# Down groups of parts two and three: four weight pairs by seven products instead of three, and another order of the products

## The chip, the cores and the metric

The kernel runs on one core of a Trainium2 chip. The metric is device time in microseconds (us), the median of three runs. All arithmetic is in float32; a float32 factor is split into a high and a low part (type fp32r), and a product of two such factors takes three matmuls: high by high, low by high, high by low. The engines that matter here: TensorE (PE) does the matmuls, ScalarE (ACT) makes the high parts by a cast, VectorE (DVE) makes the low parts by a subtraction and adds tiles, SyncE (SP) and GpSimd (POOL) issue the loads. Each engine works through its own instructions in order and waits for semaphores of the others.

## The reference

One decoder block on 256 tokens of width 2048: a half-step feed-forward network (FFN), a mixer of two kinds of heads, a second half-step FFN, a gated embedding and a last norm. Only the FFNs are touched:

```python
def swiglu(x, w_gu, w_down):
    gate, up = jnp.split(x @ w_gu, 2, axis=-1)
    return (jax.nn.silu(gate) * up) @ w_down
h = h + 0.5 * swiglu(rms_norm(h, ffn1_norm[i]), ffn1_w_gu[i], ffn1_w_down[i])
```

The inner width is 5632, which is 11 blocks of 512 columns.

## The kernel before

**Groups.** An FFN is worked through in three parts of 3, 4 and 4 inner blocks (`PARTS`). A part has one gate/up group for each of its blocks, and then two down groups, with `nb` 0 and 2; each down group makes two of the four output blocks of 512 columns from the part's inner blocks. The rows of the down weights that belong to one part come in pairs of 2 x 128 rows: 6 pairs in part one, 8 in parts two and three. A group writes four PSUM banks: two blocks of columns by two halves of the tokens.

**Plain pairs and products.** A plain pair (lines 541 to 552) is one weight tile `raw` of 128 x 1024: loaded by SP (line 74), cast by ACT to `whi` (line 77), subtracted by DVE to `wlo` (line 78), and used by 12 matmuls of 512 columns. For two blocks of columns one pair index costs two plain pairs, 24 matmuls. The first `ns` pair indices of a group are done instead by Strassen's scheme: the 2 x 2 blocks (two halves of the tokens by two rows of a pair, and two rows by two blocks of columns) take seven products instead of eight, so 7 x 3 = 21 matmuls for each pair index. `ns` is 4 for gate/up groups (`NS`), and for down groups 2 in part one and 3 in parts two and three (`NS_DOWN`).

**What a product needs.** All `ns` pairs of one product go together: its weights are one tile `R` of 128 x (512 ns), a quarter of the weights, or a sum of quarters that DVE (line 307) or an adding DMA (line 314) has made in place; ACT casts it to `shi` (line 298) and DVE subtracts to `slo` (line 299). There are two buffers each for `shi` and `slo`, so the weights of a product can only be cast once the product two places ahead has done its last matmul. Products 0, 4 and 6 take the left side as it is (4 is A12, the first half of the tokens with the second rows of the pairs). Products 1, 2, 3 and 5 take sums of left sides, `Sh` and `Sl`, which `halves` makes from the hidden blocks `hTh`, `hTl`: for down groups of parts two and three one pair index at a time (line 539), an inner block giving two indices. Behind products 0 and 1 ACT copies the result to another bank (line 347), behind products 2 and 3 ACT copies it to `part` (line 350) and DVE subtracts that from another bank (line 352).

**What sets the order.** `plan` puts the products of a group between the plain pairs of the group before it: behind plain pairs 1 to 7 of the last gate/up group of parts two and three stand the seven products of that part's first down group, in the order `SEVEN` = 0, 1, 2, 4, 3, 5, 6. Generators in `Lanes` are advanced one step behind each plain pair; they make the sums for the left sides and bring each hidden block (`down_input`) through two DMAs into `hTh` and `hTl`. In the first down group the plain pairs that use the last hidden block stand last (line 265). What is written so is then put in order by a scheduler, engine by engine, except for instructions marked `keep_in_program_order`.

Of the kernel before, what the change touches and what calls it, by code (L numbers as in the profile page):

```python
# [26 lines left out]
PARTS = ((0, 3), (3, 7), (7, 11))  # L27


NS = 4  # L30
NS_DOWN = tuple(3 if i1 - i0 == 4 else 2 for i0, i1 in PARTS)


SEVEN = (0, 1, 2, 4, 3, 5, 6)


W_IN_ORDER = (2, 0, 4, 3, 1, 5, 8, 10, 12, 9, 11, 13, 6, 7)
# [9 lines left out]
def block_kernel(ctx, tc, a, out):  # L47
# [15 lines left out]
    lanes = Lanes(4)  # L63
# [184 lines left out]
    class Group:  # L248
# [8 lines left out]
        def __init__(self, kind, part, src, quarters, ns, bank, nb=0):  # L257
            self.kind, self.part, self.src, self.ns, self.nb, self.bank = kind, part, src, ns, nb, bank
            self.quarters, self.raw, self.first = quarters, {}, False
            self.last = part == len(PARTS) - 1  # L260
            self.banks = self.follower = None
            self.plain = [(b, g) for b in range(2) for g in range(ns, len(src[0]))]
            if kind == "dn" and nb == 0:

                self.plain.sort(key=lambda x: x[1] >= len(src[0]) - 2)
            elif kind == "behind":

                self.plain.sort(key=lambda x: x[1] // 2)
            self.sums = self.all_sums()
# [20 lines left out]
        def all_sums(self):  # L290

            fp = current[0]

            def halved(j, b):
                w = self.raw[j, b]
                hi = fp.tile([P, NS, NB], F32R, tag="shi", name="shi", bufs=2)[:, 0:self.ns]
                lo = fp.tile([P, NS, NB], F32R, tag="slo", name="slo", bufs=2)[:, 0:self.ns]
                keep(nc.scalar.copy(hi, w))  # L298
                nc.vector.tensor_tensor(out=lo, in0=w, in1=hi, op=ALU.subtract)  # L299
                return hi, lo  # L300

            def keep(ins):

                return tc.keep_in_program_order(ins) if self.first == "2" else ins

            def add(x, y):
                keep(nc.vector.tensor_tensor(out=self.raw[x], in0=self.raw[x], in1=self.raw[y], op=ALU.add))  # L307

            def add_loaded(x, y):


                if self.first:
                    return add(x, y)
                nc.gpsimd.dma_start(out=self.raw[x], in_=self.quarters[y[1]][y[0]], accum_op=ALU.add)

            for i in SEVEN:
                ws = halved(*((0, 0), (0, 0), (0, 0), (0, 1), (1, 0), (1, 1), (0, 0))[i])
                if i == 0:
                    add((0, 0), (0, 1))
                    add_loaded((0, 1), (1, 1))  # L320
                elif i == 1:
                    add((0, 0), (1, 1))
                elif i == 2:
                    add_loaded((0, 0), (1, 0))
                yield ws
# [28 lines left out]
    def plan(n):  # L354


        def sources(name, blk):

            q, pairs = a[name + "q"][blk], a[name][blk]
            return [q[:, :, g, :].rearrange("j p n -> p j n") for g in range(q.shape[2])] + \  # L360
                [pairs[g] for g in range(pairs.shape[0])], q

        groups = []
        for p, (i0, i1) in enumerate(PARTS):
            for i in range(i0, i1):
                plain = PLAIN[n]
                if i < plain:
                    src = [([a[f"w_gu{n}0"][2 * i + b][g] for g in range(KD // 2)], None) for b in range(2)]
                else:
                    src = [sources("w_gu" + n, 2 * (i - plain) + b) for b in range(2)]  # L370
                groups.append(Group("gu", p, [x[0] for x in src], [x[1] for x in src], NS if i >= plain else 0,
                                    len(groups) % 2))
            for nb in (0, 2):
                src = [sources(f"w_down{n}{p}", nb + b) for b in range(2)]
                groups.append(Group("dn", p, [x[0] for x in src], [x[1] for x in src], NS_DOWN[p], len(groups) % 2, nb))
        if n == "2":
            src = [sources("w_behind", b) for b in range(2)]
            groups.append(Group("behind", len(PARTS), [x[0] for x in src], [x[1] for x in src], NS_BEHIND,
                                len(groups) % 2))
        if n == "1":  # L380

            groups[0].plain.sort(key=lambda x: x[1])
        made, carried = [], []
        for i, group in enumerate(groups):
            group.follower = follower = groups[i + 1] if i + 1 < len(groups) else None
            after = groups[i + 2] if i + 2 < len(groups) else None
            n_plain = len(group.plain)
            at, loads, carried = [], {0: carried}, []
            if follower is not None and follower.ns:
                first = 8 if not group.ns else 4 if follower.kind == "behind" else \  # L390
                    1 if group.kind == follower.kind or group.part and follower.kind == "dn" else 2
                at = [min(first + j, n_plain - 1) for j in range(7)]
                if not group.ns:
                    follower.first = n

                    loads.setdefault(max(at[0] - 5, 0), []).extend(follower.loads())
                if after is not None and after.ns:
                    *three, last = after.loads(follower)
                    for x, one in zip((4, 5, 6), three):
                        loads.setdefault(at[x], []).append(one)  # L400
                    carried = [last]
            todo = []
            for j, (b, g) in enumerate(group.plain):
                todo.append(("plain", (b, g)))
                order.append(("pair", group.src[b][g]))
                if group.kind == "behind" and g == KD // 2 - 1:
                    order.append(("pair", a["w_pp"][b]))
                for x in range(7):
                    if at and at[x] == j:
                        todo.append(("seventh", x))  # L410
                        order.append(("sum", follower))
                order.extend(loads.get(j, []))
            made.append((group, todo))
        return made
# [8 lines left out]
    def halves(kind, his, los, ns, wait=0, at_once=2):  # L423
# [19 lines left out]
        for g0 in range(0, ns, at_once):  # L443
            n = min(at_once, ns - g0)
            k0 = 2 * (g0 % 2)
            hi, lo = (x[g0 // 2][:, k0:k0 + 2 * n] for x in (his, los))
            keep = lambda ins: ins
            if g0 == 2 and n == 1:

                keep = tc.keep_in_program_order  # L450
                yield
            if n == 2:
                x = fp.tile([P, 2 * NB], F32, tag="sil", name="S")
            else:
# [14 lines left out]
    def ffn(n, nT, r, scale, next_norm, stat):  # L469
        xs = picker(*nT)  # L470
        late = callable(r)
        with tc.tile_pool(name="ffn", bufs=1) as fp:
            hTh, hTl = [], []
# [42 lines left out]
            for group, todo in ffn_plan[n]:  # L516
# [5 lines left out]
                if dn and group.nb and not group.last:  # L522
                    lanes.add(1, halves("gu", *nT, NS))
                elif dn and group.nb and group.follower:
                    lanes.add(1, halves("behind", *nxt, NS_BEHIND, 4))
                elif not dn and group.follower.kind == "dn" and not group.part:
                    lanes.add(1, halves("dn", hTh[i0:], hTl[i0:], NS_DOWN[group.part]))
                if dn and group.last and nxt is None:
                    nxt = new_nT()
                if group.banks is None:  # L530
# [1 line left out]
                for kind, one in todo:  # L532
                    if kind == "seventh":
                        follower = group.follower
                        follower.product(SEVEN[one])
                        if group.part and not dn and one == 5 and follower.kind == "gu" and \
                                follower.follower.kind == "dn":
                            p = PARTS[group.part][0]
                            lanes.add(1, halves("dn", Later(hTh, p), Later(hTl, p), NS_DOWN[group.part], 0, 1))
                        continue  # L540
                    b, g = one
                    whi, wlo = next_weights()
# [29 lines left out]
                    else:  # L572
# [7 lines left out]
                        hTl.append(tl)  # L580
                        i0, i1 = PARTS[group.part]

                        last = (3 if i1 - i0 == 4 else 2) if len(hTh) == i1 else 0
                        gen = down_input(outs, sil, th, tl, last)
                        next(gen)

# [762 lines left out]
def _layout(i):  # L1349
    f = {k: np.asarray(v) for k, v in i.items()}  # L1350
    m = {}
# [5 lines left out]
    for n in "12":  # L1357
        b = _blocks(f[f"ffn{n}_w_gu"][0])
        nb = DFF // NB
        b = np.stack([b[:nb], b[nb:]], axis=1).reshape(b.shape)  # L1360
        m[f"w_gu{n}0"] = np.ascontiguousarray(b[:2 * PLAIN[n]])
        _parted(m, f"w_gu{n}", b[2 * PLAIN[n]:], NS)
        b = _blocks(f[f"ffn{n}_w_down"][0])
        for p, (i0, i1) in enumerate(PARTS):
            _parted(m, f"w_down{n}{p}", b[:, 2 * i0:2 * i1], NS_DOWN[p])
    _parted(m, "w_behind", _blocks(f["ple_w_gate"][0])[0:2], NS_BEHIND)
    w = f["w_in"][0]
    m["w_in"] = _blocks(np.concatenate([w[:, :4096], w[:, 4112:]], axis=1))
# [29 lines left out]
```

## Time and profile before

| | us |
|---|---|
| median of 3 runs (1944.40 to 1944.83) | 1944.74 |
| the profiled execution's own time | 1945.28 |
| its span, first to last instruction | 1943.6 |
| PE busy, 8884 matmuls | 1928.1 |
| DVE busy | 1570.4 |
| ACT busy | 1164.1 |
| POOL busy | 148.4 |

A matmul of 512 columns is listed with about 0.39 us, but the next one starts 0.227 us behind it, since they overlap. The places of this text in the profiled span, for the first FFN: part two has its last gate/up group from 339.2 to 375.3 us, its first down group to 416.8 and its second to 463.0; in part three the last gate/up group runs from 586 to 622 and the first down group to 663.5. The second FFN has the same stages at 1482 to 1606 and from 1729 on. In the rows below a number in brackets at the end is the idle time of the engine just before, and the instruction that ended it.

### The profile page before, as it was taken

The page shows a single profiled execution, that of the slowest core. Times are in us where ns is not written, and L with a number is a line of the kernel's source. Part 1 is how long each engine was busy: PE and PEld are TensorE (multiplying, and loading weights), DVE is VectorE, ACT ScalarE, POOL GpSimd, SP SyncE. Part 2 cuts the span into 40 slices and gives each one's busy share as a digit, 9 for nine tenths or more (in the row PEclk, how much of TensorE's full clock was granted, in tenths as well). Part 3 has the DMA queues.
Part 4 walks back from the last instruction along what each step waited for, and adds up shares of the span by engine and source line. Part 5 has one row for each costly group of instructions (what it writes and reads, how often), then busy time and mean ns, then how long its engine had stood idle before and what let it go on. Part 6 is the DMA issues. An engine that isn't in the chain of part 4 may idle for free.

```text
span 1943.6 us, 24163 instructions
## 1 busy us (share of the span) xinstructions
PE 1928.1 (99%) x8884; PEld 1594.0 (82%) x8884; DVE 1570.4 (81%) x1703; ACT 1164.1 (60%) x1362; POOL 148.4 (8%) x226
## 2 busy tenths in 40 slices
PE   9999999999999999999999999999999999999998
PEld 7888888888888888878788888888888888888886
DVE  7879878997789766797856579899888987888865
ACT  6656666666666557664555456566556755657654
POOL 0010110000010000010100000010000100001000
PEclk9999999999999999999999999999999999999999
DMA  8778898888888765556565776788888987989764
GB/s 307 269 236 282 252 293 285 237 288 249 280 285 242 228 218 171 176 169 211 161 213 159 244 283 231 226 281 289 248 275 241 327 264 244 271 237 314 234 214 143
DMA packets 144182, 475.05 MB, mean 244 GB/s; under 512 B 19648, under 2 KB 47296, under 8 KB 129856
## 3 DMA queue, kind: packets, MB, share of 16 engines
q1 hardware_dynamic: 107200, 302.16, 44.4%
q0 software_dynamic: 25920, 160.44, 30.2%
q10 hardware_dynamic: 10944, 10.91, 1.8%
q8 instruction: 69, 1.13, 0.2%
q14 instruction: 49, 0.40, 0.1%
HBM read 451.44 MB, written 22.02 MB: 244 GB/s over the span
## 4 chain that ended last, share of the span: by engine, by line
PE 92%; DVE 5%; DMA 2%; issue 1%; ACT 0%; POOL 0%; SPq 0%; POOLq 0%; DVEq 0%; ACTq 0%
PE d L550 5%; PE d L552 5%; PE d L551 5%; PE u L551 5%; PE u L552 5%; PE u L550 5%; PE g L343 5%; PE g L342 5%; PE g L344 5%; PE g L551 4%; PE g L552 4%; PE pj L112 4%; PE pj L113 4%; PE pj L114 4%; PE g L550 4%; PE d L344 3%
## 5 line engine op out<-in xcount | busy, mean ns | idle before, releaser
L77 ACT CAST whi<-raw 128x1024 fp32r<-128x1024 f32 (+1 forms) x489 | 511.3, 1049 | 401.1 <-PE pj L114 106.6
L78 DVE TENSOR_TENSOR wlo<-raw,whi 128x1024 fp32r<-128x1024 f32 (+1 forms) x489 | 592.0, 1218 | 162.9 <-ACT whi L77 161.8
L299 DVE TENSOR_TENSOR slo<-R,shi 128x2048 fp32r<-128x2048 f32 (+2 forms) x224 | 444.9, 1989 | 132.1 <-ACT shi L298 130.1
L298 ACT CAST shi<-R 128x2048 fp32r<-128x2048 f32 (+2 forms) x224 | 373.9, 1671 | 141.5 <-DVE R L307 62.7
L112 PE MATMUL pj<-whi,nTh 128*128 128x512 f32 x448 | 179.4, 401 | 0.0
L113 PE MATMUL pj<-wlo,nTh 128*128 128x512 f32 x448 | 175.2, 391 | 1.1 <-DVE wlo L78 1.1
L114 PE MATMUL pj<-whi,nTl 128*128 128x512 f32 x448 | 174.9, 390 | 0.0
L550 PE MATMUL d<-whi,hTh 128*128 128x512 f32 x448 | 174.5, 390 | 0.0
L551 PE MATMUL d<-wlo,hTh 128*128 128x512 f32 x448 | 174.4, 389 | 0.0
L552 PE MATMUL d<-whi,hTl 128*128 128x512 f32 x448 | 173.4, 389 | 0.0
L551 PE MATMUL g<-wlo,nTh 128*128 128x512 f32 x400 | 156.6, 391 | 0.6 <-DVE wlo L78 0.6
L552 PE MATMUL g<-whi,nTl 128*128 128x512 f32 x400 | 156.0, 390 | 0.0
L551 PE MATMUL u<-wlo,nTh 128*128 128x512 f32 x400 | 155.8, 389 | 0.2 <-DVE wlo L78 0.2
L552 PE MATMUL u<-whi,nTl 128*128 128x512 f32 x400 | 155.6, 389 | 0.0
L550 PE MATMUL g<-whi,nTh 128*128 128x512 f32 x400 | 155.0, 391 | 0.6 <-ACT nTh L161 0.6
L550 PE MATMUL u<-whi,nTh 128*128 128x512 f32 x400 | 153.4, 389 | 0.0
L307 DVE TENSOR_TENSOR R<-R 128x2048 f32<-128x2048 f32 (+2 forms) x68 | 135.7, 1996 | 0.1
L113 PEld LDWEIGHTS pj<-wlo,nTh 128*128 128x128 f32 x448 | 84.2, 188 | 18.9 <-DVE wlo L78 2.7
L550 PEld LDWEIGHTS d<-whi,hTh 128*128 128x128 f32 x448 | 84.1, 188 | 18.1 <-ACT hTh L504 1.0
L552 PEld LDWEIGHTS d<-whi,hTl 128*128 128x128 f32 x448 | 84.1, 188 | 17.8
L114 PEld LDWEIGHTS pj<-whi,nTl 128*128 128x128 f32 x448 | 84.1, 188 | 17.6
L551 PEld LDWEIGHTS d<-wlo,hTh 128*128 128x128 f32 x448 | 84.1, 188 | 17.4
(332 smaller groups left out, 3447.0 us busy)
## 6 DMA issues: line engine op xcount, KB each, us to landing
raw<-in_w_gu SPq DMA_DIRECT2D x199, 512.0 KB, 5.8
raw<-in_w_down SPq DMA_DIRECT2D x112, 512.0 KB, 6.4
raw<-in_w_in SPq DMA_DIRECT2D x112, 512.0 KB, 3.4
R<-in_w_gu2q POOLq DMA_DIRECT2D x54, 1024.0 KB, 8.6
R<-in_w_gu1q POOLq DMA_DIRECT2D x48, 1024.0 KB, 8.3
raw<-in_w_out SPq DMA_DIRECT2D x32, 512.0 KB, 4.3
tT<-scr SPq DMA_DIRECT2D x22, 512.0 KB, 5.8
R<-in_w_down11q POOLq DMA_DIRECT2D x12, 768.0 KB, 7.0
```

What stands on the lines that cost most here:

```text
L77: nc.scalar.copy(hi[:, j, :], raw[:, j, :])
L78: nc.vector.tensor_tensor(out=lo[:, j, :], in0=raw[:, j, :], in1=hi[:, j, :], op=ALU.subtract)
L112: nc.tensor.matmul(outs[t], xh[:, c], whi[:, j, :], start=st, stop=False)
L113: nc.tensor.matmul(outs[t], xh[:, c], wlo[:, j, :], start=False, stop=False)
L114: nc.tensor.matmul(outs[t], xl[:, c], whi[:, j, :], start=False, stop=sp)
L298: keep(nc.scalar.copy(hi, w))
L299: nc.vector.tensor_tensor(out=lo, in0=w, in1=hi, op=ALU.subtract)
L307: keep(nc.vector.tensor_tensor(out=self.raw[x], in0=self.raw[x], in1=self.raw[y], op=ALU.add))
L344: nc.tensor.matmul(out, xl, whi[:, g, :], start=False, stop=sp, skip_group_check=True)
L550: nc.tensor.matmul(out, xh[:, c], whi[:, j, :], start=st, stop=False, skip_group_check=True)
L551: nc.tensor.matmul(out, xh[:, c], wlo[:, j, :], start=False, stop=False, skip_group_check=True)
L552: nc.tensor.matmul(out, xl[:, c], whi[:, j, :], start=False, stop=sp, skip_group_check=True)
```

## The change

`NS_DOWN` gets one number for each down group: 2, 2 in part one as before, 4, 4 in part two, 4, 3 in part three. So three down groups of each FFN take one more pair index by seven products, and two plain pairs fewer. In parts two and three the first down group uses the new order `SEVEN_DOWN` = 0, 4, 1, 2, 3, 5, 6, with A12's product second. The two sums of left sides from the second inner block are kept in program order, and the number of steps between the load of the last hidden block and its casts falls from 3 to 2 in parts two and three. The weights are laid out accordingly on the host. Line numbers behind the changed places are larger by 1 (lines 77 and 78), 2 (lines 298 to 352) or 4 (from line 456 on).

```diff
-NS_DOWN = tuple(3 if i1 - i0 == 4 else 2 for i0, i1 in PARTS)
+NS_DOWN = (2, 2), (4, 4), (4, 3)
 SEVEN = (0, 1, 2, 4, 3, 5, 6)
+SEVEN_DOWN = (0, 4, 1, 2, 3, 5, 6)
...
+            self.seven = SEVEN_DOWN if kind == "dn" and part and nb == 0 else SEVEN
...
-            for i in SEVEN:
+            for i in self.seven:
                 ws = halved(*((0, 0), (0, 0), (0, 0), (0, 1), (1, 0), (1, 1), (0, 0))[i])
...
-                src = [sources(f"w_down{n}{p}", nb + b) for b in range(2)]
-                groups.append(Group("dn", p, [x[0] for x in src], [x[1] for x in src], NS_DOWN[p], len(groups) % 2, nb))
+                src = [sources(f"w_down{n}{p}{nb // 2}", b) for b in range(2)]
+                groups.append(Group("dn", p, [x[0] for x in src], [x[1] for x in src], NS_DOWN[p][nb // 2],
+                                    len(groups) % 2, nb))
...
-            if g0 == 2 and n == 1:
+            if g0 >= 2 and n == 1:
                 keep = tc.keep_in_program_order
-                yield
+                if g0 == 2:
+                    yield
...
-                        follower.product(SEVEN[one])
+                        follower.product(follower.seven[one])
...
-                        last = (3 if i1 - i0 == 4 else 2) if len(hTh) == i1 else 0
+                        last = (6 - NS_DOWN[group.part][0] if i1 - i0 == 4 else 2) if len(hTh) == i1 else 0
```

**How the order moves on PE: the ends of products 1 and 2.** This is the last gate/up group of part two in the first FFN. Before, with three indices, the last matmuls of products 1 (into `d0`) and 2 (into `d1`) stand together, and two and a half plain pairs of the group (30 matmuls) are still to come behind them:

```order
L552 MATMUL u1_2454<-whi_2830,nTl_105 128x512
L342 MATMUL d0_2780<-shi_2727,Sh_2683 128x512
L343 MATMUL d0_2780<-slo_2728,Sh_2683 128x512
L342 MATMUL d1_2779<-shi_2792,Sh_2683 128x512
L344 MATMUL d0_2780<-shi_2727,Sl_2684 128x512
L343 MATMUL d1_2779<-slo_2793,Sh_2683 128x512
L344 MATMUL d1_2779<-shi_2792,Sl_2684 128x512
L550 MATMUL u0_2453<-whi_2830,nTh_101 128x512
```

Now, with a fourth index, they end inside the last plain pair but one, whose weights are `whi_2883`; behind them come two of its matmuls and the last plain pair, `whi_2922`:

```order
L555 MATMUL u0_2453<-wlo_2884,nTh_102 128x512
L344 MATMUL d0_2787<-shi_2802,Sh_2683 128x512
L345 MATMUL d0_2787<-slo_2803,Sh_2683 128x512
L344 MATMUL d1_2786<-shi_2837,Sh_2683 128x512
L345 MATMUL d1_2786<-slo_2838,Sh_2683 128x512
L556 MATMUL u0_2453<-whi_2883,nTl_106 128x512
L554 MATMUL u1_2454<-whi_2883,nTh_102 128x512
L346 MATMUL d0_2787<-shi_2802,Sl_2684 128x512
L346 MATMUL d1_2786<-shi_2837,Sl_2684 128x512
L555 MATMUL u1_2454<-wlo_2884,nTh_102 128x512
L556 MATMUL u1_2454<-whi_2883,nTl_106 128x512
L554 MATMUL u0_2453<-whi_2922,nTh_102 128x512
```

What moved: the two products now end with the fourth sum of left sides, with 14 plain matmuls of the group behind them. Products 3, 5 and 6 (36 matmuls, weights `shi_2876`, `shi_2915`, `shi_2956`) stand behind all but the last of these, with no plain matmul between them; before, the twelve matmuls of the group's last plain pair (`whi_2902`) were spread among products 3, 5 and 6: one inside product 3, one behind it, eight inside product 5 and two ahead of product 6.

**At the end of the burst on PE.** The change's row of the next product (`shi_3000`, the second down group's first) stands inside product 6, ahead of the first use of `slo_2957`:

```order
L346 MATMUL d0_2787<-shi_2915,Sl_2684 128x512
L344 MATMUL d1_2786<-shi_2956,hTh_2085 128x512
L344 MATMUL d1_3090<-shi_3000,hTh_2085 128x512
L345 MATMUL d1_2786<-slo_2957,hTh_2085 128x512
L346 MATMUL d1_2786<-shi_2956,hTl_2086 128x512
```

Before, product 6 begins behind the rest of that plain pair and runs through:

```order
L344 MATMUL d0_2780<-shi_2895,Sl_2684 128x512
L551 MATMUL u1_2454<-wlo_2903,nTh_102 128x512
L552 MATMUL u1_2454<-whi_2902,nTl_106 128x512
L342 MATMUL d1_2779<-shi_2933,hTh_2085 128x512
L343 MATMUL d1_2779<-slo_2934,hTh_2085 128x512
L344 MATMUL d1_2779<-shi_2933,hTl_2086 128x512
```

What moved: two plain matmuls went from between products 5 and 6, and one matmul that waits for another cast came in.

**On ACT, the same stretch after the change.** The rows begin with the casts of the last two plain pairs ahead of the fourth sum:

```order
L78 CAST whi_2922<-raw_2921 128x1024
L78 CAST whi_2963<-raw_2962 128x1024
L468 CAST Sh_2683<-S_2777 128x512
L349 COPY d1_2788<-d0_2787 128x512
L300 CAST shi_2876<-R_2584 128x2048
L352 COPY part_2912<-d1_2786 128x512
L300 CAST shi_2915<-R_2625 128x2048
L78 CAST whi_2983<-raw_2982 128x1024
L78 CAST whi_3035<-raw_3034 128x1024
L352 COPY part_2953<-d1_2786 128x512
L300 CAST shi_2956<-R_2548 128x2048
L300 CAST shi_3000<-R_2880 128x2048
```

What moved: the copies that end products 1, 2 and 3 (`d1_2788`, `part_2912`, `part_2953`) each stand just ahead of the cast of product 3's, 5's or 6's weights, as before, but these casts are 2048 wide instead of 1536, and the fourth `Sh` stands ahead of them all.

More of the change, by code (lines that the diff above doesn't have):

```diff
@@ L526, in ffn @@
                 elif not dn and group.follower.kind == "dn" and not group.part:
-                    lanes.add(1, halves("dn", hTh[i0:], hTl[i0:], NS_DOWN[group.part]))
+                    lanes.add(1, halves("dn", hTh[i0:], hTl[i0:], NS_DOWN[group.part][0]))
                 if dn and group.last and nxt is None:
@@ L538, in ffn @@
                             p = PARTS[group.part][0]
-                            lanes.add(1, halves("dn", Later(hTh, p), Later(hTl, p), NS_DOWN[group.part], 0, 1))
+                            lanes.add(1, halves("dn", Later(hTh, p), Later(hTl, p), NS_DOWN[group.part][0], 0, 1))
                         continue
@@ L1364, in _layout @@
         for p, (i0, i1) in enumerate(PARTS):
-            _parted(m, f"w_down{n}{p}", b[:, 2 * i0:2 * i1], NS_DOWN[p])
+            for j in range(2):
+                _parted(m, f"w_down{n}{p}{j}", b[2 * j:2 * j + 2, 2 * i0:2 * i1], NS_DOWN[p][j])
     _parted(m, "w_behind", _blocks(f["ple_w_gate"][0])[0:2], NS_BEHIND)
```

## The prediction

> **What bounds the kernel now.** I read the page first, its busy shares and the chain that ended last.
>
> ```profile
> PE 1928.1 (99%) x8884; PEld 1594.0 (82%) x8884; DVE 1570.4 (81%) x1703; ACT 1164.1 (60%) x1362; POOL 148.4 (8%) x226
> PE 92%; DVE 5%; DMA 2%; issue 1%; ACT 0%; POOL 0%; SPq 0%; POOLq 0%; DVEq 0%; ACTq 0%
> ```
>
> PE sets the time, so a matmul taken away is worth its pitch as long as nothing else is late. Whether it is, is read from the stages. The table of windows has, for each stretch, the time and the busy time of PE, PEld, DVE, ACT and POOL, the granted clock and the DMA share. Its rows are part two's last gate/up group, first and second down group, then part three's first down group.
>
> ```profile
> 339.20:375.30 36.10, 36.10 (x160) 29.67 (x159) 32.64 (x40) 22.12 (x26) 3.87 (x6) 1.00 0.80 230
> 375.30:416.80 41.50, 41.50 (x184) 34.37 (x184) 39.64 (x38) 26.51 (x27) 4.05 (x7) 1.00 0.96 321
> 416.80:463.00 46.20, 46.20 (x204) 37.82 (x204) 40.20 (x34) 27.05 (x23) 3.97 (x6) 1.00 0.82 258
> 622.00:663.50 41.50, 41.50 (x184) 34.37 (x184) 34.99 (x33) 25.14 (x29) 1.85 (x3) 1.00 0.77 232
> ```
>
> PE never pauses in them (its busy time is the whole window), but DVE has only 3.5 us idle in the first row and 1.9 in the second. It is the engine next in line, and the change gives it more to do. The timeline of the first stretch shows how near DVE already is:
>
> ```profile
> 352.21 1.19 DVE L78 TENSOR_TENSOR wlo<-raw,whi 128x1024 fp32r<-128x1024 f32 x1
> 353.45 0.50 PE L551 MATMUL g<-wlo,nTh 128*128 128x512 f32 x1
> ```
>
> The low part ends at 353.40 and PE takes it at 353.45. So at this point, with the sums for the left sides being made between the weights, there is no slack: what DVE gets on top ahead of it, PE waits for.
>
> **The gain.** From the timeline of PE, near that group's end:
>
> ```profile
> 370.38 0.39 PE L344 MATMUL d<-shi,Sl 128*128 128x512 f32 x1
> 375.36 0.39 PE L343 MATMUL d<-slo,hTh 128*128 128x512 f32 x1
> ```
>
> The 22 matmuls from the first row on take 4.98 us, 0.2267 each. A pair index by products costs 21 matmuls instead of 24, three indices for each FFN are changed, so 18 go: **4.08 us**, 0.21% of the time.
>
> **What it puts on DVE and ACT.** The groups of part two's three stages, by shape:
>
> ```profile
> L298 ACT CAST shi<-R 128x1536 fp32r<-128x1536 f32 x13 | 19.3, 1482 | 3.8 <-PE d L344 2.1 <-PE g L344 1.7
> L298 ACT CAST shi<-R 128x2048 fp32r<-128x2048 f32 x8 | 15.3, 1915 | 4.9 <-PE g L344 2.0 <-PE u L344 1.7 <-PE d L344 1.0
> L350 ACT COPY part<-d 128x512 f32<-128x512 f32 x4 | 2.3, 586 | 3.4 <-PE d L344 3.4
> L78 DVE TENSOR_TENSOR wlo<-raw,whi 128x1024 fp32r<-128x1024 f32 x28 | 34.0, 1222 | 1.4 <-ACT whi L77 1.4
> L299 DVE TENSOR_TENSOR slo<-R,shi 128x1536 fp32r<-128x1536 f32 x13 | 22.7, 1753 | 1.4 <-ACT shi L298 1.3
> L299 DVE TENSOR_TENSOR slo<-R,shi 128x2048 fp32r<-128x2048 f32 x8 | 18.3, 2291 | 7.0 <-ACT shi L298 7.0
> L307 DVE TENSOR_TENSOR R<-R 128x1536 f32<-128x1536 f32 x4 | 7.0, 1746 | 0.0
> L307 DVE TENSOR_TENSOR R<-R 128x2048 f32<-128x2048 f32 x3 | 6.9, 2287 | 0.0
> L462 DVE TENSOR_TENSOR S<-S 128x128 f32<-128x128 f32 x11 | 2.9, 292 | 0.0
> L465 DVE TENSOR_TENSOR Sl<-S,Sh 128x512 fp32r<-128x512 f32 x3 | 2.1, 693 | 0.7 <-ACT Sh L464 0.7
> L456 DVE TENSOR_TENSOR S<-hTh,hTl 128x512 f32<-128x512 f32 x2 | 1.4, 690 | 0.0
> ```
>
> With a fourth index a product's subtraction costs 2.29 instead of 1.75 us on DVE, an addition of weights 2.29 instead of 1.75, its cast 1.92 instead of 1.48 on ACT. The fourth sum of left sides adds one L456, four L462 and one L465, 2.55 us. The last gate/up group gets 6 subtractions and 2 additions more dear by 0.54 and that sum, so DVE 32.6 + 4.3 + 2.6 = 39.5 us, while PE has 21 matmuls more, 36.1 + 4.8 = 40.9. The first down group of part two: DVE 39.6 - 2 x 1.22 + 9 x 0.54 = 42.1, PE 180 matmuls or 40.8. The second: DVE 40.2 - 2.4 = 37.8, PE 40.8. So on average DVE is just full, and it is the order that decides. An average does not say when a single tile is ready, so I walk through the engines' orders. The four places (the last gate/up group of parts two and three, in both FFNs) have the same listed order of plain pairs and products up to the burst of products 3, 5 and 6; I walk through the first, on the clock of the trace before, in which both programs are equal up to these rows:
>
> ```profile
> 336.05 0.69 DVE L456 TENSOR_TENSOR S<-hTh,hTl 128x512 f32<-128x512 f32 x1
> 346.40 0.39 PE L342 MATMUL d<-shi,hTh 128*128 128x512 f32 x1
> 343.25 0.69 DVE L465 TENSOR_TENSOR Sl<-S,Sh 128x512 fp32r<-128x512 f32 x1
> 343.85 0.29 DVE L462 TENSOR_TENSOR S<-S 128x128 f32<-128x128 f32 x1
> 342.39 0.75 DVE L482 SCALAR_TENSOR_TENSOR sil<-u,rstd,sil 128x512 f32<-128x512 f32 x1
> 346.45 1.29 DVE L505 TENSOR_TENSOR hTl<-tT,hTh 128x512 fp32r<-128x512 f32 x2
> 349.32 0.71 DVE L487 STREAM_TRANSPOSE tb<-sil 128x512 f32<-128x512 f32 x1
> ```
>
> **First wait, 0.7 us.** Up to the low part of the first `u` pair DVE has, from 336.05 on, 29 instructions: 3 subtractions and 2 additions of 2.29, 3 low parts of 1.22, 3 first sums of 0.69, 10 small ones of 0.29, 2 `Sl` of 0.69, 2 `sil` of 0.75, 2 transposes of 0.70, 2 `hTl` of 0.69. That is 25.7 us, less 0.09 each for overlap (343.25 to 343.85 is 0.60 for a 0.69), 23.2; the first subtraction waits 0.4 for its wider cast. Ready at 359.8. PE needs it 56 matmuls after 346.40, at 359.1.
>
> **Second wait, 1.3 us.** Product 1's last matmul stands 104 behind 346.40, so with 0.7 lost at 370.7, and ends at 371.05. Only then may ACT copy its result and reuse the buffer for product 3's cast. How long that chain takes is seen before, between products 3 and 6:
>
> ```profile
> 370.80 0.59 ACT L350 COPY part<-d 128x512 f32<-128x512 f32 x1 [0.78 <-PE d L344]
> 371.28 1.48 ACT L298 CAST shi<-R 128x1536 fp32r<-128x1536 f32 x1
> 372.80 1.76 DVE L299 TENSOR_TENSOR slo<-R,shi 128x1536 fp32r<-128x1536 f32 x1 [0.27 <-ACT shi L298]
> ```
>
> Product 3's last matmul ended at 370.77; copy, cast and subtraction followed at once, to 374.56, and PE came at 375.36, because ten plain matmuls stood between. With the wide tiles the chain is 0.5 + 1.92 + 0.04 + 2.29 = 4.75, so 371.05 becomes 375.8. PE's first use is 17 matmuls behind 370.7, at 374.5. Here product 1 now ends late, since it needs the fourth sum; before, it ended 30 plain matmuls ahead of the group's end.
>
> **Third wait, 2.0 us.** Product 3 has 11 matmuls left and ends at 378.5. Product 5's subtraction ends at 378.7, 0.1 late. Product 6's cast waits for product 3's end and its copy, 379.0 to 380.9; DVE, behind a low part, `d` and `sil`, subtracts from 381.0 to 383.3. Meanwhile product 5, 12 matmuls, is over at 381.2. Nothing can fill in: the plain pairs of the group are used up, and those of the down group need the third hidden block, whose casts stand behind these two on ACT and whose low part stands behind the subtractions on DVE. And the matmul of the next product that stands inside product 6 waits for a cast that gets its buffer at product 5's end, 381.3 + 1.9 = 383.2. PE wanted it at 381.4, so 1.9; with the 0.1 of product 5, 2.0. What is queued behind does not add to it: the third hidden block's low part follows on DVE behind the next product's subtraction, one `sil` and one addition of weights (2.2 + 0.7 + 2.2 + 0.6), at 389.1, and PE, with 10 matmuls of product 6, 4 of the down group and 11 of its next product to do first, comes at 389.3. Together **4.0 us** a place, 16.0 for four.
>
> Bounds for a place: if DVE is somewhere ahead of my walk and only the last chain counts, 4.75 from product 3's end against 14 matmuls, 3.2, it is 1.6; if the first down group's deficit on DVE comes on top, 42.1 - 40.8 = 1.3, it is 5.3. I take 4.0, where the walk leads: on the trace before the same sums of durations give the `wlo` of 352.21 to within 0.1 us.
>
> **A12's product second** issues nothing new. It gives the left sides' sums the time of a product and a plain pair more, which is why product 4 itself waits for nothing. Its price is that the addition of two quarters by DMA behind product 2 is issued one place later: behind product 2's subtraction, 363.7 in the walk, so it lands by 374.2 at the 10.5 us below, 5 us before product 6's cast. That cover also holds the kept order and the step taken off `last`.
>
> **The rest.** In part two's first down group my walk on DVE reaches product 3's subtraction and the last hidden block's low part 0.3 us behind PE; I take 0.3 for each FFN, 0.6, with 0 and 1.3 as ends. In part three that group has DVE 35.0 - 2.4 of 36.0 us, and no wait. Two loads could become late, with A12's quarter and with the last hidden block:
>
> ```profile
> 335.29 0.54 POOL L279 DMA_DIRECT2D R<-in_w_down11q  x1 [4.93 <-DVE slo L299]
> R<-in_w_gu1q POOLq DMA_DIRECT2D x5, 1024.0 KB, 10.5
> 382.74 1.30 DVE L487 STREAM_TRANSPOSE tb<-sil 128x512 f32<-128x512 f32 x2
> 390.53 0.33 SPq L498 DMA_DIRECT2D tT<-scr  x1
> DMA to landing us min/median/max: 5.9/5.9/5.9
> ```
>
> A12's quarter is loaded last, but at the slower landing of a 1 MB tile in this stretch it is there at 345.8; its cast and subtraction, 4.2 us, must begin by 347.8. The last hidden block lands 12.4 us behind its transposes (384.0 to 396.4); these end near 392 in my walk, so it lands at 404.5, and PE wants the block at about 410. SP issues two 512 KB loads fewer in such a group and POOL the same six with 256 KB more each, so neither queue gets a longer row of issues. All this is covered by 2 us or more; were the cover gone, it would be 1 to 2 us a place.
>
> **Sum.** -4.1 + 16.0 + 0.6 = +12.5 us. On the profiled execution's 1945.28 that is 1957.8; the median lies 0.54 lower, so **1957 us**.
>
> **Rivals.** *The waits eat the gain and no more (1941 to 1948).* For it: DVE's 3.5 us idle in the first window, and that PE stood still nowhere at 96% of DVE in the second. If the walk places product 1's end 3 us too late, a place costs the first 0.7 and little else, 4 x 1.0 - 4.1, about 1944.7. Against: the 353.45 row has no slack to begin from. 15%.
>
> *Faster (1940.7).* The cover holds whole: if product 3's subtraction lands within the 17 matmuls behind product 1's end, and product 6's within 14, PE loses nothing and all 4.08 us are kept. For it: ACT is busy 22 of 36 us. Against: the chain's 4.75 is over the 3.5 that PE has at the first of these points and over the 3.2 at the second, and with two buffers the cast cannot begin before the earlier product has ended. 8%.
>
> *Later transfers too (1963).* The hidden block or the quarter lands 1 to 2 us late in each place, +6. For it: a DMA share of 0.96 in the second window. 11%.
>
> *Clock (1964).* A wait of PE might be followed by a slower stretch.
>
> ```profile
> 924.00:928.00 4.00, 2.84 (x17) 2.26 (x16) 3.90 (x8) 1.04 (x1) 0.00 (x0) 1.00 0.39 133
> ```
>
> Against: in the mixer PE idles 1.2 of 4 us at a granted 1.00. [...] 3%. [...]
>
> That the change is not what it says is excluded by the listed orders: PE has 18 rows fewer.
>
> **How the numbers follow.** Forecast 63%, with its own range from the bounds: 4 x 1.6 - 4.1 = +2.3, so 1947, and 4 x 5.3 + 2.6 - 4.1 = +19.7, so 1964. The point is the likeliest case's. A measurement of this kernel can tell 0.2%, 3.9 us, from no change: faster means below 1940.9, slower above 1948.6. Faster 0.07 and within 0.17 share the first two rivals and the forecast's lowest end; slower 0.76 is the rest of the forecast and the last two rivals. The range leaves out the fast cases, under 20%, and takes in the bounds: 1945 to 1964.
>
> **What would show it.** PE's idle time ahead of the first matmul with `slo` (line 345 there), 1.3 us in product 3 and about 2 in product 6, ended by DVE `slo`, or by ACT `shi` for the next product, in each of the four places, and 0.7 ended by DVE `wlo` ahead of them; on ACT, copy and cast close behind one another in that stretch; 8866 matmuls. Wrong, if PE has no gap between the last `u` matmul and the second down group's first product, or if the gap is ended by a DMA.

## The result, and the profile after

The changed kernel takes 1959.64 us (median of 4 runs, 1959.4 to 1960.69), the kernel before 1944.78 in the same comparison. The ratio is 1.0078, with a 95% interval from 1.0063 to 1.0092: slower. The profiled execution took 1959.83 us, 14.55 more than that of before.

The page's busy times of the changed kernel, and the engines of its chain that ended last:

```profile
PE 1930.4 (99%) x8866; PEld 1587.5 (81%) x8866; DVE 1593.5 (81%) x1715; ACT 1171.7 (60%) x1354; POOL 148.3 (8%) x226
PE 89%; DVE 6%; DMA 2%; issue 1%; ACT 1%; POOL 0%; SPq 0%; POOLq 0%; DVEq 0%; ACTq 0%
```

The 18 matmuls are gone (8866 for 8884), and yet PE's share of the chain fell from 92 to 89%. What PE waits for is listed by the table of PE's waits; its columns are what waited, for what, us in total, times, and the longest. Its first three rows are new; the kernel before has no wait of PE at all between 300 and 690 us:

```profile
PE d L344 <- ACT shi L300: 6.2, 4, 1.8
PE d L345 <- DVE slo L301: 4.5, 4, 1.1
PE u L555 <- DVE wlo L79: 1.9, 4, 0.5
```

Each comes four times, once in each of the four places: 12.6 us of idle PE. The windows show it by stage, first part two's last gate/up group in the first FFN, then the end of part three's; the columns are those of the prediction's windows:

```profile
338.70:382.70 44.00, 41.18 (x178) 32.48 (x176) 39.78 (x48) 27.41 (x28) 3.41 (x5) 1.00 0.79 240
609.00:634.00 25.00, 22.20 (x92) 16.95 (x93) 20.76 (x23) 17.68 (x19) 2.36 (x4) 1.00 0.80 252
```

Before, PE was busy through all of the window; now 2.8 us are missing in each, though DVE and ACT have idle time too. So no engine is full over these stretches: PE, ACT and DVE wait for one another in turn. The three waits of the first place on PE's timeline:

```profile
359.23 0.50 PE L555 MATMUL u<-wlo,nTh 128*128 128x512 f32 x1 [0.47 <-DVE wlo L79]
375.65 0.50 PE L345 MATMUL d<-slo,Sh 128*128 128x512 f32 x1 [1.11 <-DVE slo L301]
375.99 0.39 PE L346 MATMUL d<-shi,Sl 128*128 128x512 f32 x1
383.22 0.50 PE L344 MATMUL d<-shi,hTh 128*128 128x512 f32 x1 [1.75 <-ACT shi L300]
```

The ring behind the second and third waits, on ACT's and DVE's timelines of the same stretch:

```profile
370.87 0.57 ACT L349 COPY d<-d 128x512 f32<-128x512 f32 x1 [1.98 <-PE d L346]
371.36 1.91 ACT L300 CAST shi<-R 128x2048 fp32r<-128x2048 f32 x1
...
378.48 0.59 ACT L352 COPY part<-d 128x512 f32<-128x512 f32 x1 [1.04 <-PE d L346]
378.96 1.91 ACT L300 CAST shi<-R 128x2048 fp32r<-128x2048 f32 x1
381.26 1.90 ACT L300 CAST shi<-R 128x2048 fp32r<-128x2048 f32 x1 [0.39 <-PE d L346]
...
373.30 2.29 DVE L301 TENSOR_TENSOR slo<-R,shi 128x2048 fp32r<-128x2048 f32 x1 [3.07 <-ACT shi L300]
380.91 4.58 DVE L301 TENSOR_TENSOR slo<-R,shi 128x2048 fp32r<-128x2048 f32 x2
```

ACT waits for product 1's end on PE (370.87), copies, casts for product 3 (371.36 to 373.27); DVE, idle for 3.07 us, subtracts to 375.59; PE goes on at 375.65. The ring turns once more behind product 3's end (378.48) and product 5's (381.26).

**Where 18.6 us went.** The time is 14.55 up and 4.08 were saved, so 18.6 were lost. The idle time is 12.6. A wait cost more than its idle here: the matmul behind it starts 0.34 later instead of 0.2267 (375.65 to 375.99), and the matmul itself starts about 0.17 later than the idle says (in the third experiment's rows below 2.44 behind the one ahead of it, less the 0.2267, for an idle of 2.04). That is 0.28 for each of the 12, 3.4. The rest are small delays that PE's row does not show as idle, but that of its weight loads (PEld) does: in the first place, in part three's first down group, and in part two's:

```profile
368.94 0.19 PEld L344 LDWEIGHTS d<-shi,Sh 128*128 128x128 f32 x1 [0.32 <-ACT Sh L468]
655.11 0.19 PEld L344 LDWEIGHTS d<-shi,Sh 128*128 128x128 f32 x1 [0.44 <-ACT shi L300]
655.62 0.19 PEld L554 LDWEIGHTS d<-whi,hTh 128*128 128x128 f32 x1 [0.33 <-ACT hTh L508]
408.05 0.19 PEld L554 LDWEIGHTS d<-whi,hTh 128*128 128x128 f32 x1 [0.33 <-ACT hTh L508]
```

By the starts of the matmuls around them the delays in the two down groups cost 0.57 and 0.33 us in each FFN, and another 0.29 stands behind part three's third wait, for the third hidden block's cast: 2.4 in all. The first row is a short wait for the fourth sum itself; with three more delays of 0.05 to 0.11 it costs 0.28 a place, 1.1 in all. So 12.6 + 3.4 + 2.4 + 1.1 = 19.5 us were lost, and the two traces, laid side by side matmul by matmul, give 19.8 for the four stages. The time shows only 18.6, because this execution was 1.3 us faster where the two programs are alike: 0.5 ahead of the first place (the matmul of the prediction's 346.40 starts at 345.87), and 0.8 behind the last, where only the trace before has a wait of 0.5 (`gt` for `wlo`).

### The profile page after: what moved, and what is told of

Same layout as the page of the kernel before. It is cut to its first block, busy times and chain, and to the rows that moved or that the text cites. A ratio compares the mean times of both kernels' runs of the same rounds, so it can differ in the third digit from the quotient of the medians.

```text
span 1958.1 us, 24108 instructions
## 1 busy us (share of the span) xinstructions
PE 1930.4 (99%) x8866; PEld 1587.5 (81%) x8866; DVE 1593.5 (81%) x1715; ACT 1171.7 (60%) x1354; POOL 148.3 (8%) x226
## 4 chain that ended last, share of the span: by engine, by line
PE 89%; DVE 6%; DMA 2%; issue 1%; ACT 1%; POOL 0%; SPq 0%; POOLq 0%; DVEq 0%; ACTq 0%
PE d L554 5%; PE d L556 5%; PE d L555 5%; PE g L345 4%; PE g L344 4%; PE g L346 4%; PE u L555 4%; PE u L556 4%; PE u L554 4%; PE pj L113 4%; PE pj L114 4%; PE pj L115 4%; PE g L555 4%; PE g L556 4%; PE g L554 4%; PE d L345 3%
## 5 line engine op out<-in xcount | busy, mean ns | idle before, releaser
L78 ACT CAST whi<-raw 128x1024 fp32r<-128x1024 f32 (+1 forms) x477 | 499.1, 1050 | 397.9 <-PE pj L115 104.1
L79 DVE TENSOR_TENSOR wlo<-raw,whi 128x1024 fp32r<-128x1024 f32 (+1 forms) x477 | 577.7, 1216 | 165.0 <-ACT whi L78 163.6
L301 DVE TENSOR_TENSOR slo<-R,shi 128x2048 fp32r<-128x2048 f32 (+2 forms) x224 | 467.1, 2088 | 125.9 <-ACT shi L300 122.0
L300 ACT CAST shi<-R 128x2048 fp32r<-128x2048 f32 (+2 forms) x224 | 392.1, 1752 | 160.7 <-DVE R L309 91.5
L554 PE MATMUL d<-whi,hTh 128*128 128x512 f32 x400 | 156.0, 392 | 0.1
L555 PE MATMUL d<-wlo,hTh 128*128 128x512 f32 x400 | 155.1, 389 | 0.0
L556 PE MATMUL d<-whi,hTl 128*128 128x512 f32 x400 | 154.7, 389 | 0.0
L113 PEld LDWEIGHTS pj<-whi,nTh 128*128 128x128 f32 x448 | 84.2, 188 | 16.6
L345 PE MATMUL g<-slo,nTh 128*128 128x512 f32 x234 | 91.3, 390 | 0.0
L346 PE MATMUL g<-shi,nTl 128*128 128x512 f32 x234 | 91.1, 389 | 0.0
```

Of the source, the lines that this page charges most:

```text
L78: nc.scalar.copy(hi[:, j, :], raw[:, j, :])
L79: nc.vector.tensor_tensor(out=lo[:, j, :], in0=raw[:, j, :], in1=hi[:, j, :], op=ALU.subtract)
L113: nc.tensor.matmul(outs[t], xh[:, c], whi[:, j, :], start=st, stop=False)
L345: nc.tensor.matmul(out, xh, wlo[:, g, :], start=False, stop=False, skip_group_check=True)
L346: nc.tensor.matmul(out, xl, whi[:, g, :], start=False, stop=sp, skip_group_check=True)
L554: nc.tensor.matmul(out, xh[:, c], whi[:, j, :], start=st, stop=False, skip_group_check=True)
```

## The experiments

The theory: the fourth sum of left sides makes products 1 and 2 end late, and since `shi` and `slo` have two buffers each, copy, cast and subtraction of the products behind them start only then. Its rivals: DVE is simply full; the wider tiles are too slow by themselves; loads or the new product order do the harm.

**1. The fourth sum is made, but not used.**

```diff
+            g = min(g, 2) if kind == "dn" else g
             return sh[:, g, j, t, :], sl[:, g, j, t, :]
```

> The changed kernel, but the products of the down groups take the third pair index's left sum where they should take the fourth's, so the output is another; the fourth sum is still made, on the same engines and at its price, and nothing waits for it. My theory: products 1 and 2 end late because their fourth pair index waits for that sum, and with two buffers everything behind their ends (copy 0.5, cast 1.92, subtraction 2.29) is late too. It expects the second wait (1.1 us ahead of product 3's slo) and the third (1.3 to 1.75 us in product 6) to go, and the first (0.5 us, DVE's lag ahead of wlo) to stay: 1944.8 - 4.1 + 4 x 0.6 + 0.6 = 1944, between 1942 and 1948. Rival 'DVE is full': its work is the same, so the waits stay and the time is 1957 to 1960. Rival 'wide tiles': casts and subtractions of 2048 columns are what is too slow, also 1957 to 1960.

Measured: 1949.58 us (10 runs, 1946.73 to 1951.37), 1.0022 of before [1.0013, 1.0031]; 10 us below the changed kernel. PE's waits:

```profile
PE u L556 <- DVE wlo L79: 2.1, 5, 0.5
PE d L346 <- DVE hTl L510: 1.4, 2, 1.1
PE d L557 <- DVE hTl L510: 1.0, 1, 1.0
```

The second and third waits are gone with the dependence, at the same work on DVE (1593.6 us busy, 1593.5 in the changed kernel); the first is as it was. So DVE's load is not what made them. The expectation still missed: 1949.6 is above its 1948. Three waits came up for the low part of a hidden block (`hTl`), 2.4 us with none before. One (1.0) stands behind a place, where PE now arrives earlier. The other two (1.1 and 0.3) stand ahead of a place's first wait, where nothing was gained yet: there the block was late in this execution, and why is not shown.

**2. The fourth sum is not made either.** The line of the first experiment stays.

```diff
-        for g0 in range(0, ns, at_once):
+        for g0 in range(0, min(ns, 3) if kind == "dn" else ns, at_once):
...
-            if not g0 % 2 + n == 1 or g0 + n == ns:
+            if not g0 % 2 + n == 1 or g0 + n == (min(ns, 3) if kind == "dn" else ns):
```

> As the run before, and the fourth sum isn't made either: DVE does 2.55 us less in each of the four places, ACT one cast of 512 columns less; the output is another. My theory expects the first wait (0.5 us) to go too: 1944.8 - 4.1 + 0.6 = 1941, up to 1946 if a part of the first wait comes from the wider tiles. If it is as long as the run before, the fourth sum costs by where its result is needed and not by its work. Rival 'wide tiles': 1957 to 1960 in both.

Measured: 1950.13 us (8 runs), 1.0026 [1.0016, 1.0037], as the run before. Its waits:

```profile
PE d L557 <- DVE hTl L510: 2.2, 2, 1.7
PE u L556 <- DVE wlo L79: 1.9, 4, 0.5
```

Expected was that the first wait goes too, and at most 1946; the wait stays, 1.9 us in four places, and the time is 4 us above. So the fourth sum costs by where its result is needed, and its work costs nothing that these runs can tell (the ten of the first experiment and the eight of this one both scatter over about 5 us). What stands ahead of the first wait, on DVE in the changed kernel, explains that:

```profile
353.15 2.28 DVE L301 TENSOR_TENSOR slo<-R,shi 128x2048 fp32r<-128x2048 f32 x1
355.55 2.28 DVE L309 TENSOR_TENSOR R<-R 128x2048 f32<-128x2048 f32 x1
357.95 1.22 DVE L79 TENSOR_TENSOR wlo<-raw,whi 128x1024 fp32r<-128x1024 f32 x1
363.44 0.68 DVE L460 TENSOR_TENSOR S<-hTh,hTl 128x512 f32<-128x512 f32 x1
```

The fourth sum begins at 363.44, behind this `wlo`; ahead of it stand the wide subtraction and addition. The first wait belongs to the wider tiles; run 4 below, with three indices again in part three, has it in the two part-two places alone.

**3. A third buffer for the high part.** No new room is taken: product 3 borrows the buffer of A12's quarter, which is free since that product is second. (`halved` gets the number `i` of the product for this.)

```diff
...
-                hi = fp.tile([P, NS, NB], F32R, tag="shi", name="shi", bufs=2)[:, 0:self.ns]
+                hi = (fp.tile([P, NS, NB], F32R, tag=self.home[1, 0], name="shi") if i == 3 and self.seven != SEVEN else
+                      fp.tile([P, NS, NB], F32R, tag="shi", name="shi", bufs=2))[:, 0:self.ns]
...
```

> The changed kernel; the high part of product 3's weights in the three changed down groups goes to the buffer that A12's quarter has left free (its product is second), so casts run one product further ahead. Nothing is left out. My theory: behind product 1's end only the subtraction, 2.29 us, is left instead of 4.75, and PE has 17 matmuls, 3.85 us, so the second wait (1.1) goes; product 6's cast then hangs on product 2's end, not 3's, and its subtraction of 2.29 behind product 3's end stands against 14 matmuls, 3.2, so the wait for slo there goes as well; what may stay is the first wait (0.6) and the one for the next product's shi (0 to 1.9). 1944.8 - 4.1 + 0.6 + 4 x 0.6 = 1943.7 to 1951, I say 1946. Rival 'DVE is full': a cast earlier does not help, 1956 to 1960. Rival 'the load that follows in the borrowed buffer': it is issued a few us later, and if it then lands late PE waits for a DMA, 1960 or more.

Measured: 1960.48 us (4 runs), 1.0076 [1.0059, 1.0093]: no gain. By the total alone the theory would have fallen; the rows say otherwise. First PE's waits, then the load and the cast at the first place, and PE:

```profile
PE d L345 <- ACT shi L301: 6.9, 4, 2.7
...
375.75 0.55 POOL L281 DMA_DIRECT2D R<-in_w_down111q  x1 [2.27 <-PE d L347]
382.82 1.90 ACT L301 CAST shi<-R 128x2048 fp32r<-128x2048 f32 x1 [1.68 <-DMA R<-in_w_down111q]
...
382.33 0.39 PE L347 MATMUL d<-shi,hTl 128*128 128x512 f32 x1
384.77 0.50 PE L345 MATMUL d<-shi,hTh 128*128 128x512 f32 x1 [2.04 <-ACT shi L301]
```

No wait for `slo` is left among PE's. In their place PE waits, in the two part-two places (2.0 and 2.7), for the second down group's first cast, which waits for a load that the borrowed buffer held back to 375.75; in the changed kernel this load is issued at 350.85. That is the last rival of the expectation. The other two waits for `shi`, 1.0 each, are in part three's first down group. The total also holds two slow stretches of PE behind the long waits (granted clock 0.50, last section).

**4. Part two alone** (`NS_DOWN = (2, 2), (4, 4), (3, 3)`).

> Only part two has four pairs by products; part three's both down groups are as before, with A12's product second still in both. My theory: the loss is made in the four places, two of which are undone. Each part-two place loses 3.3 us in the three waits, 0.4 for the starts behind them and 0.5 in the first down group: 1944.8 - 2.7 + 2 x 4.7 = 1951.5, between 1950 and 1953.5. Rival 'the down groups of part three': if it sits in them rather than in the places, more than 6 us of the 14.9 go away, below 1948. Rival 'the product order': it stays in both parts and the time stays above 1955.

Measured: 1954.65 us (4 runs), 1.0056 [1.0041, 1.0071], 1.1 above the range. Its waits:

```profile
PE d L344 <- ACT shi L300: 3.5, 2, 1.8
PE d L345 <- DVE slo L301: 2.2, 2, 1.1
PE d L346 <- DVE hTl L509: 1.1, 1, 1.1
```

The waits of two places are there unchanged, those of the other two are gone: the loss sits in the places. The excess has a row in the profiled execution (1953.91): the second hidden block of part two in the second FFN came late (1.1, and 0.8 for its high part just ahead), as in the first experiment.

**5. The third buffer, and another home for the load.** The load that is needed first goes to the buffer that product 3's own quarter leaves.

```diff
-            free = [last.home[q] for q in ((1, 0), (0, 1), (1, 1), (0, 0))] if last else ["R0", "R1", "R2", "R3"]
+            free = [last.home[q] for q in (((1, 0), (0, 1), (1, 1), (0, 0)) if last.seven == SEVEN else
+                                           ((0, 1), (1, 0), (1, 1), (0, 0)))] if last else ["R0", "R1", "R2", "R3"]
```

> The run with the third buffer again, and the second down group's A11 quarter, the first that is needed, is loaded into the buffer that product 3's own quarter leaves (free 2.8 us before the borrowed one in that run). Nothing is left out. Theory: the run with the third buffer only traded the two waits for slo for one for this load (issued at 375.75, landed as the cast began at 382.82, PE idle 2.04 to 384.77). Issued at about 372.9 it lands 2.8 us earlier, PE's idle 2.0 to 2.7 us there goes, and with it the slow stretch behind it (granted clock 0.60 to 0.81): 2.5 to 4 us in each of the two part-two places, so 1960.5 - 2 x 3 = 1954, between 1951 and 1957. Rival 'the DMA queue is full there': the load lands as late as before, and the time stays at 1959 to 1961.

Measured: 1951.04 us (5 runs), 1.0032 [1.002, 1.0045]: 9.4 less than the third experiment and 8.6 less than the changed kernel, with the whole computation done. Its load and PE's waits:

```profile
373.14 0.56 POOL L281 DMA_DIRECT2D R<-in_w_down111q  x1 [9.35 <-DVE slo L302]
...
PE d L345 <- ACT shi L301: 2.1, 2, 1.0
PE u L556 <- DVE wlo L79: 1.4, 3, 0.5
```

The load is issued 2.6 us earlier and the wait in part two goes. The two that are left for `shi` are in part three's first down group. So the waits 2 and 3 vanish by either road, products 1 and 2 ending early (1 and 2) or a third buffer (5): they are made by both together.

**6. The old product order.**

```diff
-            self.seven = SEVEN_DOWN if kind == "dn" and part and nb == 0 else SEVEN
+            self.seven = SEVEN
```

> The changed kernel with the product order of before: A12's product stands fourth again, between products 2 and 3. Nothing is left out. Theory: the products behind the late ends of products 1 and 2 are then four instead of three, 47 product matmuls in one row on PE instead of 36, each link of the chain 4.2 us of cast and subtraction against 12 matmuls, 2.7 us, and A12's buffer comes free later for the second group's first load: 1.5 to 2.5 us more a place, 1966 to 1970, I say 1967. Rival 'the order does nothing': 1959 to 1961. Rival 'A12 second is what harms' (its quarter's load, the wide cast between products 0 and 1): below 1957.

Measured: 1974.53 us (4 runs), 1.0162 [1.0145, 1.0178]. The direction is the theory's, the size is 4.5 above its range, and the rows are not those it named:

```profile
PE d L344 <- ACT Sh L468: 7.9, 4, 3.0
PE d L345 <- DVE slo L301: 6.5, 4, 1.6
PE g L555 <- DVE wlo L79: 5.3, 6, 1.2
PE d L344 <- ACT shi L300: 4.4, 5, 1.1
```

The largest is a wait for `Sh`: with product 1 second, PE stands at a sum of left sides itself. A12 second is worth 15 us to the changed kernel, most of all by the time it gives those sums.

**7. The new order alone**, with three pairs everywhere (`NS_DOWN = (2, 2), (3, 3), (3, 3)`).

> Only the order of the products is changed: three pair indices by products everywhere, as before, with A12's product second in the first down groups of parts two and three. Nothing is left out. Theory: it issues nothing new and no matmul waits, 1944.8, between 1943.8 and 1946. Rival 'A12's quarter is needed too early' (loaded last of the four) or 'the addition by DMA behind product 2 comes too late for product 6': 1 to 3 us a place, 1949 or more.

Measured: 1946.47 us (11 runs), 1.0006 [0.9998, 1.0015]: not to be told from no change, 0.5 above the range. Its one new wait is `d` for `hTl`, 2.3 us in two places: plain pairs on the third hidden block come up earlier than before. Whether the order costs 1 or 2 us stays open.

**8. Four pairs in part two's second down group alone**, old order (`NS_DOWN = (2, 2), (3, 4), (3, 3)`; the fourth sum is made with the others, `max(NS_DOWN[group.part])`).

> Four pairs by products in the second down group of part two alone, whose products stand behind 20 plain pairs of the first group; product order and all other groups as before. Nothing is left out. Six matmuls of each FFN's 9 go, so 12 of 18 are not saved: 6 x 0.2267 = 1.4 us less in all. Theory: the fourth sum is harmless where it is ready long before product 1 needs it, so no wait comes: 1943.4, between 1942.5 and 1945. Rival 'DVE is full': the wider tiles bring 9 x 0.54 - 2 x 1.22 = 2.4 us more for DVE into stages in which it has 1.9 and 6 us idle, and PE waits for it, 1946 to 1950.

Measured: 1942.97 us (11 runs), 0.999 [0.9981, 0.9999]: 1.84 us faster than before. PE has no wait between 300 and 690 us, and DVE makes the fourth sum in the very stretch of the first place (336 to 376):

```profile
L469 DVE TENSOR_TENSOR Sl<-S,Sh 128x512 fp32r<-128x512 f32 x4 | 2.8, 688 | 0.7 <-ACT Sh L468 0.7
```

The same sum at the same spot harms nothing where the next 20 plain pairs stand ahead of its use.

**9. The second groups of parts two and three.** `(3, 4)` for both, and in an FFN's last group two more steps for the norm:

```diff
-                            lanes.advance(0)
+                            for _ in range(3 if group.ns == 4 and b == 0 else 1):
+                                lanes.advance(0)
```

> Four pairs by products in the second down groups of parts two and three, three in the first ones, product order as before; in the last group of an FFN the steps of the norm behind it are taken two places earlier, since two plain pairs fewer stand there. Nothing is left out. 12 matmuls go, 12 x 0.2267 = 2.7 us. Theory: as in part two alone (measured 1942.97, 1.8 below before for 6 matmuls), the fourth sum is ready long before it is needed, so 1944.8 - 2.7 = 1942.1, less the same surplus 1941.7, between 1940.5 and 1943. Rival 'the end of the FFN': with two plain pairs fewer behind its products the last group covers less of the norm and of what follows, and 1 to 3 us are lost there in each FFN: 1943.5 to 1948.

Measured: 1942.5 us (11 runs; before 1944.22 beside it), 0.999 [0.9981, 0.9999]: 1.7 faster, not 2.7. A part of the rest shows behind the first FFN: one wait more of the mixer's first matmuls (0.6 us) than in the kernel before, whose row has 1.1 in 3.

```profile
PE pj L114 <- DVE wlo L79: 1.7, 4, 0.5
```

This and the run before are both ahead of the two kernels of this text; between them nothing can be told.

## Why the prediction was right

Forecast: 1957, slower, by three waits in four places. Measured: 1959.64. Step by step, with 0.28 for the restart added to the idle time, since the prediction counted to where PE would have stood:

- **Gain 4.08:** the 18 matmuls went. Right.
- **First wait 0.7:** 0.47 + 0.28 = 0.75. The row is right, DVE ahead of `wlo`, and so are its parts, since the walk put the wide tiles ahead of it, not the fourth sum (run 2). The size is right in part by a slip: the walk's own terms, 336.05 + 23.2 + 0.4, end at 359.65, not at 359.8, and give 0.55.
- **Second wait 1.3:** 1.11 + 0.28 = 1.39. The walk had product 1's end at 371.05, and ACT copied its result at 370.87; the subtraction was to end at 375.8 and ended at 375.59. Read so, the walk looks closer than it was: the trace after stood 0.53 ahead of the trace before at this stage. On one clock product 1's end and this subtraction came about 0.3 later than walked, and the third wait's rows 0.5; the restarts and small delays make up for most of that. The waits themselves are differences and stay as they are.
- **Third wait 2.0:** 1.75 + 0.28 = 2.03 in part two, with subtraction (380.91 to 383.2, said 381.0 to 383.3) and cast (done 383.16, said 383.2) as walked. In part three it is 1.6; one walk had been taken for both.
- **Sum of the places 16.0:** 12.6 + 3.4 = 16.0. That it agrees to the tenth is luck: the first two waits were a little longer than said, and part three's third wait was shorter.
- **The rest 0.6, the mis-sized term:** 3.5 by rows, 2.4 in and ahead of the down groups and 1.1 of small delays in the places; the 1.3 us by which this execution was faster elsewhere bring the total nearer to the forecast, and that is luck too. Part two's first down group was to cost 0.3 and costs 0.33, but not for the reason given: the walk had DVE late with the low part, and what is late is ACT with the high part. Part three's was to have no wait and costs 0.57, of which 0.18 is a wait for a product's own weights, and behind its third wait PE loses 0.29. In all three the hidden block's cast stands straight behind a cast of weights on ACT. The prediction looked at when the last block lands, not at what is ahead of it on ACT.
- **A12's quarter:** no wait of PE or ACT for it. Right; and run 6 showed what the prediction only said in a clause, that the new order keeps PE from waiting for the left sums.
- **Cover of 2 us for the last hidden block:** for its landing it was there (405.5 in part two, and PE wanted the block at 407.8), but ACT used it up: at 405.56 it began a cast of weights, and the block's cast came behind it.

```profile
405.56 1.92 ACT L300 CAST shi<-R 128x2048 fp32r<-128x2048 f32 x1
407.37 1.15 ACT L508 CAST hTh<-tT 128x512 fp32r<-128x512 f32 x2
```

- **Cover of the second and third blocks:** the prediction gave the third 0.2 us (389.1 against 389.3) and said nothing of the second. In runs 1 to 5, 1.6 to 2.5 us of waits for `hTh` or `hTl` came up. Where they are for the third block (runs 1 to 4, and run 7), PE stands less ahead of it than in the changed kernel. Where they are for the second (runs 1, 4 and 5), they come ahead of the place's first wait; runs 2 and 7 have none there, and what makes the block late is open.
- **Rivals.** "The waits eat the gain and no more" and "faster" supposed that the walk places the ends too late: on one clock the rows are 0.3 to 0.5 us later than the walk, so it was not too late. "Later transfers": none that PE waits for in the changed kernel. "Clock": no run shows the 7 us that lead to its 1964. The granted clock was 1.00 in the four places and behind them (383.30 to 387.30 in the first), so nothing was lost to it here; in run 5 one slow stretch made eight matmuls 1.6 us longer together (last section).

## What to carry to other kernels

Where two engines hand buffers to a third in a ring, busy shares say little: DVE was 81% busy, and idle for 3.07 us right before the subtraction that PE waited for. Ask which input of a product is ready last and how many products stand behind it in a row without other work; then either move the saving to where that input is long ready (run 8), or break the ring with another buffer and look at whose load the buffer was (runs 3 and 5).

## What was not expected of the hardware

Behind some waits PE ran at about half its rate. Two rows of PE's timeline in run 3 show it (starts 0.42 apart instead of 0.2267). In windows cut to where the granted clock changes it is 0.50 throughout. First run 3, one window ahead of its first slow stretch, that stretch and its second one; then run 5's slow stretch:

```profile
387.01 0.63 PE L555 MATMUL d<-whi,hTh 128*128 128x512 f32 x1
387.43 0.63 PE L556 MATMUL d<-wlo,hTh 128*128 128x512 f32 x1
```

```profile
383.11:386.52 3.41, 1.73 (x6) 1.24 (x7) 1.77 (x1) 2.65 (x3) 0.00 (x0) 1.00 0.99 410
386.52:389.93 3.41, 3.41 (x9) 2.64 (x8) 3.41 (x4) 0.00 (x0) 0.00 (x0) 0.50 0.55 221
1536.81:1540.22 3.41, 3.41 (x8) 2.48 (x8) 3.41 (x3) 0.79 (x2) 0.00 (x0) 0.50 0.86 353
```

```profile
1496.48:1499.89 3.41, 3.41 (x10) 2.66 (x9) 3.41 (x4) 2.16 (x2) 0.00 (x0) 0.50 0.26 107
```

In run 6, two windows in which the clock stayed; and two of the changed kernel, the wait and what is behind it:

```profile
618.44:621.85 3.41, 2.06 (x10) 1.36 (x8) 0.84 (x1) 0.77 (x1) 0.00 (x0) 1.00 0.96 382
621.85:625.26 3.41, 2.56 (x11) 2.10 (x12) 1.83 (x2) 1.42 (x4) 0.00 (x0) 1.00 1.00 382
```

```profile
380.03:383.44 3.41, 1.66 (x8) 1.06 (x7) 3.29 (x4) 3.02 (x3) 0.00 (x0) 1.00 0.91 363
383.30:387.30 4.00, 4.00 (x18) 3.31 (x19) 4.00 (x3) 0.91 (x2) 0.54 (x1) 1.00 0.87 316
```

The granted clock fell behind an idle of 2.04 us and one of 2.7 (run 3), of 0.58 and 1.09 with two matmuls between (run 5), and of 2.97 (run 6, where it was 0.67 on average from 1781 to 1785 us); it stayed at 1.00 behind 2.21 (run 6, up to 622.70) and behind 1.75 (the changed kernel, up to 383.22). So the length of a wait alone does not decide: the two of run 5 come to 1.67 us, less than the single waits of 2.21 and 1.75 that changed nothing. What decides is not shown by these runs. Each of the three slow stretches listed is 3.41 us long; in that of run 5, eight matmuls took 0.2 more each, 1.6 us.
